# Gate and up products of a SwiGLU feed-forward by Strassen's seven block products, in a two-layer diffusion step on one Trainium2 core

## Chip, core and metric

The kernel runs on one core of one Trainium2 chip. The metric is the device time of one execution in microseconds (us). The engines are named as the profile names them: PE (TensorE, matrix products), DVE (VectorE), ACT (ScalarE), POOL (GpSimd), SP (the engine whose queue issues the DMAs).

## What is computed

The reference runs a backbone of two layers over 128 context tokens and 512 latent tokens of width 1024. A layer has adaptive modulation, a token mixer of four kinds of heads, and a SwiGLU feed-forward of inner width 2816 between two RMS norms. Only the feed-forward matters here:

```python
D_FF = -(-8 * D_MODEL // (3 * 256)) * 256            # 2816
...
h2 = modulate(rmsnorm(x, g_pre_ffn))                 # 640 tokens x 1024, both groups of tokens
f = (silu(h2 @ w_ffn_gate) * (h2 @ w_ffn_up)) @ w_ffn_down
x = x + gate * rmsnorm(f, g_post_ffn)
```

All of it is in 32-bit floating point, with the same weights for both groups of tokens.

## The kernel before

Activations lie with features on the 128 partitions and the 640 tokens along the row, cut into two halves of 320 (`HW`). A factor of a matrix product is held as two tiles, `hi` (the value rounded to the fast format fp32r) and `lo` (the rest), and a product is three passes, hi·hi, hi·lo, lo·hi (`PASSES`). One "k" of a product (128 of the depth) is thus three matmuls of 128x128 by 320 columns, and a full depth of 1024 is 24.

**Feed-forward.** The 2816 inner features are 22 tiles of 128, taken in `GROUPS` of 4, 3, 3, 4, 4 and 4. For a tile, `ev_ffn` makes for each half the gate product (24 matmuls), SiLU on ACT, the up product (24), and `ev_act` multiplies on DVE and splits the result into hi and lo (`act`). After the tiles of a group, `dn` adds the group's share of the down projection to the running sum `z` (8 output tiles, 2 halves, 3 matmuls per inner tile), which DVE evicts (`ev_dn`). The first group runs half 0 of all its tiles before half 1, since half 1 of `h` comes later; the last group keeps two tiles and its down products for a pass by halves, so that half 0 can go through `boundary` (norm, residual, norm and modulation for the next layer) while PE works on half 1.

```python
PASSES = ((0, 0), (0, 1), (1, 0))
...
for gi, gn in enumerate(GROUPS):
    ...
    for k in range(early):
        hg, hu = stream.next(), stream.next()
        for half in range(2):
            yield from ev_ffn(hg, hu, acts[k], half)
        stream.done(hg, hu)
```

**Weights.** The class `Stream` goes through a fixed list `items`. A 512 KB tile is loaded into one of three `raw` buffers and split by `split` into an `hl` tile (hi by a cast on ACT or DVE, lo by a subtraction on DVE or POOL), in one of 3 + 5 buffers. `feed` splits ahead as long as buffers are free; `next` hands a split tile to the products and `done` gives it back. Products accumulate in five PSUM tiles (`acc_tile`, `wide[0] = 5`).

**The order.** The whole program is one list that a recording layer writes: `drive` steps the main line `bulk` and a set of side lanes, and `Clock` keeps an estimate of when each engine is free. `vg` and `copy` choose the engine (DVE or POOL, DVE or ACT) by that estimate. So each engine's order is fixed when the program is built.

**Modulation weights.** In layer 0 a side lane (`mod_slots`) loads 28 MB in pieces of 1 MB (`mraw`) and lets PE make 28 small products from them (`mod_mm`, 8 matmuls in the order, `mps`), two at a time, in between the matmuls of the feed-forward; `mod_end` follows one turn later.

All engine operations come from the recording layer's `call` and so have one line in the profile, L232 (L234 in the order of the changed kernel); they are told apart by tile names.

Of the kernel before, what the change touches and what calls it, by code (L numbers as in the profile page):

```python
# [17 lines left out]
KT = 8  # L18
# [117 lines left out]
BIAS_CP = -200.0  # L136
BIAS_START = (-2000.0, 2000.0)
# [195 lines left out]
def emit(ctx, tc, a, o):  # L333
# [186 lines left out]
    def mod_lane(n):  # L520
        for _ in range(n):
            l, c = modq.pop(0)
            rawlim[0] = 1
            while stream.nd - stream.ns > 1:
                yield POLL
            raws = mod_dma(l, c)
            yield clock.done(raws) + 500.0
            tb = mod_mm(raws)
            rawlim[0] = NRAW
            yield  # L530
            mod_end(l, c, tb)
            yield

    def mod_slots(n):

        mine = [modq.pop(0) for _ in range(n)]
        tbs = []
        for i in range(0, n, 2):
            two = mine[i:i + 2]
            while live[0] + 2 * len(two) > NSLOT:  # L540
                yield POLL
            raws = [[u5([128, 4, 256], "mraw") for _ in range(2)] for _ in two]
# [6 lines left out]
            tbs = [(*lc_, mod_mm(r)) for lc_, r in zip(two, raws)]  # L549
            free(2 * len(two))  # L550
        yield
        for t in tbs:
            mod_end(*t)


    ext = [None]
    items = []
    for l in range(DEPTH):
        for c, u in [(c, u) for c in ((0, 1, 2) if l == 0 else (0, 2, 1)) + (3, 4, 5, 6, 7) for u in range(2)] + [(9, 0), (8, 0), (8, 1), (9, 1), (10, 0), (10, 1)]:
            k, n = (4, 256) if c in VCH else (KT, 128)  # L560
            items.append((a["win"][l, c, u].rearrange("p (k n) -> p k n", n=n), k, n, int(l > 0 and (1 <= c <= 2 or (c == 3 and u == 1)))))
        for c in range(8):
            items.append((a["wout"][l, c], KT, 128, int(c >= 3)))
        kb = 0
        for gi, gn in enumerate(GROUPS):
            last = gi == len(GROUPS) - 1
            for k in range(2 * gn):
                items.append((a["wgu"][l, 2 * kb + k], KT, 128, int(k == 3 or k >= 6) if last else int(k >= 3)))
            t = a["wdn"].tensor
            for m in range(0, 8, 2):  # L570
                off = l * DFF * D + 128 * kb * D + m * 128 * gn * 128
                src = bass.AP(t, off, [[gn * 128, 128], [128 * gn * 128, 2], [1, gn * 128]])
                items.append((src, 2 * gn, 128, int(m < 6) if last else int(m >= 2)))
            kb += gn

    class Stream:


        def __init__(self):
            self.raw, self.hl, self.where = {}, {}, {}  # L580
            self.nd = self.ns = self.nu = 0
            self.limit = 0
            self.used = [0, 0]

        def load(self):
            while self.nd < self.limit and self.nd < len(items) and self.nd - self.ns < rawlim[0]:
                src, kt, n, _ = items[self.nd]
# [5 lines left out]
        def split(self, at_once=False):  # L593
            _, kt, n, where = items[self.ns]
            self.used[where] += 1
            raw = self.raw.pop(self.ns)
            hl = (ext[0] if where else ring).tile([128, 2, kt, n], F32R, tag="hl", name="hl", bufs=NHL[where])
# [4 lines left out]
            self.ns += 1  # L602
            self.load()

        def free(self):
            where = items[self.ns][3]
            return self.used[where] < NHL[where] and (not where or ext[0] is not None)

        def feed(self):

            self.load()
            if self.ns < self.nd and self.free():
                now = clock.now()
                if clock.avail(self.raw[self.ns]) <= now + AHEAD and (
# [3 lines left out]
        def next(self):  # L618
            self.load()
            while self.ns <= self.nu:  # L620
                assert self.free()
# [10 lines left out]
    NHL = (3, 5)  # L632
# [726 lines left out]
    def boundary(half, yt, sqs, xls, out_dma, nxt):  # L1359
# [32 lines left out]
        if nxt:  # L1392
# [8 lines left out]
            yield from skewed(ended(pre(k)) for k in range(KT))  # L1401
        free(2)


    def bulk():
# [117 lines left out]
        for l in range(DEPTH):  # L1523
# [97 lines left out]
            ext[0] = None  # L1621
            wide[0] = 2
            bias[0] = BIAS_MIX
            pctx.close()
# [108 lines left out]
            fctx = ExitStack()  # L1733

            def scanned():
# [3 lines left out]
                ext[0] = clock.pool(fctx.enter_context(tc.tile_pool(name=f"f{l}", bufs=1)))  # L1739
                wide[0] = 5  # L1740
# [43 lines left out]
            xls = yield from residual(0, xsrc)  # L1784
            spawn(boundary(0, yt, ssqs[0], xls, xn, (l, 2, hk, ("h2", l))))
# [5 lines left out]

            def second(l=l, yt=yt, ssqs=ssqs, xls=xls, xn=xn):
                yield from boundary(1, yt, ssqs[1], xls, xn, (l, 2, hk, ("h2", l)))
                free(5)

# [248 lines left out]
```

## Time and profile before

| | |
|---|---|
| median of 3 runs | 1710.83 us (1710.33 to 1711.54) |
| the profiled execution | 1710.81 us, of which its span 1708.7 us |
| mean granted TensorE clock | 0.988 |
| PE busy | 1640.4 us (96%) |
| DVE busy | 959.7 us (56%) |
| ACT busy | 602.1 us (35%) |
| POOL busy | 228.9 us (13%) |
| DMA | 188.14 MB, mean 110 GB/s |

The span runs from the first to the last instruction; 2.1 us of the execution lie outside it. Matmuls overlap in the pipe, so the busy mean of one (313 ns) is not its share of the time; that is read from the start times of neighbours in the timeline. Layer 0 reaches to about 880 us and layer 1 to the end; in each, the mixer comes first and the feed-forward fills the second part.

### The profile page before, as it was taken

The page shows a single profiled execution, that of the slowest core. Times are in us where ns is not written, and L with a number is a line of the kernel's source. Part 1 is how long each engine was busy: PE and PEld are TensorE (multiplying, and loading weights), DVE is VectorE, ACT ScalarE, POOL GpSimd, SP SyncE. Part 2 cuts the span into 40 slices and gives each one's busy share as a digit, 9 for nine tenths or more (in the row PEclk, how much of TensorE's full clock was granted, in tenths as well). Part 3 has the DMA queues.
Part 4 walks back from the last instruction along what each step waited for, and adds up shares of the span by engine and source line. Part 5 has one row for each costly group of instructions (what it writes and reads, how often), then busy time and mean ns, then how long its engine had stood idle before and what let it go on. Part 6 is the DMA issues. An engine that isn't in the chain of part 4 may idle for free.

```text
span 1708.7 us, 31121 instructions
## 1 busy us (share of the span) xinstructions
PE 1640.4 (96%) x12784; PEld 1539.0 (90%) x12784; DVE 959.7 (56%) x2032; ACT 602.1 (35%) x1322; POOL 228.9 (13%) x280
## 2 busy tenths in 40 slices
PE   4999999999999999999979998998999999999996
PEld 2888988998999999999979986788999999999996
DVE  5488767696334444343484588775962434343356
ACT  5346655564210101011443466655642110101022
POOL 0200142032000000000233000330320000100012
PEclk9999999999999999999989998999999999999998
DMA  9332221554755621222241311104412222222022
GB/s 370 130 127 92 93 88 63 179 164 151 265 179 204 219 87 63 86 67 76 90 152 53 100 46 41 56 33 130 161 56 90 90 69 99 74 74 75 25 93 93
DMA packets 79997, 188.14 MB, mean 110 GB/s; under 512 B 7632, under 2 KB 38256, under 8 KB 79856
## 3 DMA queue, kind: packets, MB, share of 16 engines
q1 hardware_dynamic: 79856, 186.17, 32.2%
q8 instruction: 100, 1.64, 0.4%
q14 instruction: 41, 0.34, 0.1%
HBM read 173.42 MB, written 12.71 MB: 109 GB/s over the span
## 4 chain that ended last, share of the span: by engine, by line
PE 87%; DVE 7%; ACT 3%; issue 1%; DMA 1%; POOL 1%; SPq 0%; ACTq 0%; DVEq 0%; POOLq 0%
PE acc L232 68%; PE acct L232 6%; PE mps L232 3%; DVE z L232 1%; PE nsp L232 1%; DVE hl L232 1%; PE nps L232 1%; PE rops L232 1%; PE gdps L232 1%; PE ntp L232 1%; PE nops L232 1%; PE gaps L232 1%; ACT r L232 1%; PE lrp L232 1%; DVE gE L232 1%
## 5 line engine op out<-in xcount | busy, mean ns | idle before, releaser
L232 PE MATMUL acc<-h,hl 128*128 128x320 f32 x6336 | 977.9, 313 | 18.1 <-ACT h L232 9.3
L232 PEld LDWEIGHTS acc<-h,hl 128*128 128x128 f32 x6336 | 936.7, 188 | 43.6 <-issue 15.9
L232 PE MATMUL acc<-act,hl 128*128 128x320 f32 x2112 | 315.1, 310 | 1.3 <-DVE act L232 1.2
L232 PEld LDWEIGHTS acc<-act,hl 128*128 128x128 f32 x2112 | 310.4, 188 | 4.8 <-issue 2.1
L232 ACT ACTIVATE sg<-acc 128x320 f32<-128x320 f32 x88 | 38.4, 436 | 592.6 <-PE acc L232 592.5
L232 DVE TENSOR_TENSOR sg<-sg,acc 128x320 f32<-128x320 f32 x88 | 42.9, 487 | 360.3 <-PE acc L232 335.8
L232 DVE TENSOR_TENSOR hl<-raw,hl 128x1024 fp32r<-128x1024 f32 (+1 forms) x178 | 214.3, 1226 | 9.8 <-ACT hl L232 7.1
L232 POOL TENSOR_TENSOR hl<-raw,hl 128x1024 fp32r<-128x1024 f32 (+1 forms) x18 | 41.2, 2289 | 724.9 <-ACT hl L232 723.8
L232 ACT ACTIVATE hl<-raw 128x1024 fp32r<-128x1024 f32 (+1 forms) x118 | 118.6, 1030 | 51.9 <-PE acc L232 44.1
L232 PE MATMUL acct<-hl,h 128*128 128x256 f32 x960 | 133.4, 291 | 0.0
L232 PEld LDWEIGHTS acct<-hl,h 128*128 128x128 f32 x960 | 119.9, 191 | 9.1 <-issue 6.4
L232 DVE TENSOR_TENSOR z<-z,acc 128x320 f32<-128x320 f32 x160 | 74.5, 484 | 86.3 <-PE acc L232 86.2
L232 DVE CAST hl<-raw 128x1024 fp32r<-128x1024 f32 (+1 forms) x78 | 53.6, 687 | 16.8 <-PE acc L232 14.7
L232 POOL TENSOR_TENSOR nB<-nT,cst 128x248 f32<-128x248 f32 (+2 forms) x32 | 19.8, 620 | 279.3 <-DVE nsp L232 147.3
L232 PE MATMUL mps<-mraw,ct 128*32 128x256 f32 x768 | 49.1, 386 | 0.7 <-DVE modb L232 0.6
L232 POOL TENSOR_TENSOR ssqz<-ssqz,sq 128x320 f32<-128x320 f32 x34 | 32.6, 957 | 112.3 <-ACT sq L232 109.4
L232 DVE TENSOR_TENSOR act<-sg,act 128x320 fp32r<-128x320 f32 x88 | 43.3, 492 | 3.0
L232 ACT ACTIVATE qbd<-gE 32x256 f32<-32x256 f32 (+1 forms) x80 | 30.6, 382 | 37.5 <-DVE gE L232 34.4
L232 DVE CAST act<-sg 128x320 fp32r<-128x320 f32 x88 | 38.1, 432 | 3.1
L232 PEld LDWEIGHTS mps<-mraw,ct 128*32 128x32 f32 x768 | 24.7, 110 | 13.8 <-issue 2.8
L232 POOL TENSOR_TENSOR h<-xl,h 128x320 fp32r<-128x320 f32 x32 | 29.8, 944 | 46.2 <-DVE h L232 22.8
L232 DVE STREAM_TRANSPOSE modb<-mps 128x256 f32<-128x256 f32 x48 | 21.1, 445 | 18.9 <-PE mps L232 18.8
(252 smaller groups left out, 1508.1 us busy)
## 6 DMA issues: line engine op xcount, KB each, us to landing
mraw<-in_wmod SPq DMA_DIRECT2D x96, 512.0 KB
raw<-in_wgu SPq DMA_DIRECT2D x88, 512.0 KB
raw<-in_win SPq DMA_DIRECT2D x44, 512.0 KB
raw<-in_wdn SPq DMA_DIRECT2D x32, 512.0 KB
raw<-in_wout SPq DMA_DIRECT2D x16, 512.0 KB
xl<-xd SPq DMA_DIRECT2D x12, 640.0 KB
raw<-in_wdn SPq DMA_DIRECT2D x16, 384.0 KB
xd<-y SPq DMA_DIRECT2D x32, 160.0 KB
```

The costliest lines, as they stand in the source:

```text
L232: x = fn(*args, **kw)
```

## The change

Gate and up of one feature tile together are a 2x2 block matrix (gate and up as the two blocks of features, the depth of 1024 in two halves) times a 2x2 block matrix of `h` (depth halves by token halves). For 16 of the 22 tiles of a layer (all of groups 2 to 5 and the first two of the last group) the eight block products are replaced by seven (`seven`), each over a depth of 512, that is 4 k or 12 matmuls.

- **Sums of weights.** A tile now has four split tiles in place of two: gate (`plain`), the second half of up (`second`, 512 wide, tile `hu`), the four sums and differences of halves (`sums`: four `raw<-raw` operations of 128x512, in place, then a split), and the last form of up (`plain`). Buffers are 3 + 3 + 2 half ones in this stage (`hpool("b", 3)`).
- **Sums of `h`.** `sums_of_h` makes four differences of 320-token blocks in the `xl` tiles, splits three into `th` tiles and writes the fourth over the half-1 columns of `h` for the first four k, once the first group is done with them. `second_block` puts the old contents back before half 1 of the last two tiles.
- **Evictions.** `seven` evicts each product to SBUF: a copy and seven additions on DVE (`u`, `sg`), SiLU from SBUF, and `act` as before.
- **Pools.** The split buffers outside the ring are taken anew at three points of a layer (`hpool` "a", "b", "c").
- **Modulation weights** are loaded and multiplied one at a time instead of in pairs, from two buffers of the new pool, after the first group.

```diff
-                        hg, hu = stream.next(), stream.next()
-                        for half in range(2):
-                            yield from ev_ffn(hg, hu, acts[k], half)
-                        stream.done(hg, hu)
+                        yield from seven(acts[k])
...
+            def product(w, k0, x):
+                ps = acc_tile()
+                for k in range(4):
+                    for i, (wi, xi) in enumerate(PASSES):
+                        PE.matmul(ps, lhsT=w[:, wi, k0 + k, :], rhs=x(xi, k), start=(k == 0 and i == 0), stop=(k == 3 and i == 2))
+                    yield
+                return ps
...
+                hg = stream.next()
+                ps = yield from product(hg, 0, b11)
+                copy(p, ps, BIAS_SNAP)
+                ps = yield from product(hg, 4, b21)
+                stream.done(hg)
+                add(s0, p, ps)
+                S.activation(out=s0, in_=s0, func=AF.Silu)
+                hu, hs = stream.next(), stream.next()
+                ps = yield from product(hs, 0, t2)
+                add(p, p, ps)
+                hs2 = stream.next()
+                ps = yield from product(hs2, 4, t1)
+                add(s1, p, ps)
+                ps = yield from product(hs2, 0, t3)
+                stream.done(hs2)
+                add(p, p, ps)
+                add(u1, s1, ps)
+                ps = yield from product(hu, 0, t4)
+                stream.done(hu)
+                add(p, p, ps)
+                act(s0, p, ac, h0)
+                ps = yield from product(hs, 4, b22)
+                stream.done(hs)
+                add(s1, s1, ps)
+                S.activation(out=s1, in_=s1, func=AF.Silu)
+                act(s1, u1, ac, h1)
...
+                g, u = self.raw[srcs[0]], raw
+                (g1, g2), (u1, u2) = ((t[:, 0:KT // 2], t[:, KT // 2:]) for t in (g, u))
+                for out, x, y, op in ((u2, u1, u2, ALU.add), (u1, g1, u1, ALU.subtract), (g1, u2, g1, ALU.subtract), (g2, g2, g1, ALU.subtract)):
+                    vg(out, x, y, op, BIAS_SUM)
+                raw = g
...
-            for lc_, r in zip(two, raws):
-                for q in range(2):
-                    dma(out=r[q], in_=a["wmod"][lc_[0], lc_[1], q])
-            yield max(max(clock.done(r) for r in raws) + 500.0, clock.now() + 2 * MODGAP)
+            raws = mod_dma(*lc_, hx[0], 2)
+            yield max(clock.done(raws) + 500.0, clock.now() + MODGAP)
```

Over the whole program PE gets 384 matmuls fewer (6336 products of `h` become 5952, of which 1152 read `th`); DVE's order grows from 2035 to 2513 operations, ACT's from 1285 to 1359, POOL's from 286 to 334, and SP's stays at 476.

**PE, a Strassen tile in layer 0** (`h_123` to `h_130` are the eight depth tiles of `h`, `th` the sums, `mraw` modulation weights). Before:

```order
L232 MATMUL acc<-h_130,hl 128x320 x3
L232 MATMUL acc<-h_123,hl 128x320 x3
L232 MATMUL mps_6407<-modb,cst 32x4 x4
L232 MATMUL mps_6413<-modb,cst 32x4 x4
L232 MATMUL mps<-mraw,ct 32x256 x16
L232 MATMUL acc<-h_124,hl 128x320 x3
L232 MATMUL acc<-h_125,hl 128x320 x3
L232 MATMUL acc<-h_126,hl 128x320 x3
```

Now, from the third product of a tile to the last:

```order
L234 MATMUL acc<-th,hl 128x320 x24
L234 MATMUL mps_6511<-modb,cst 32x4 x4
L234 MATMUL mps<-mraw,ct 32x256 x8
L234 MATMUL acc<-h_123,hl 128x320 x3
L234 MATMUL acc<-h_124,hl 128x320 x3
L234 MATMUL acc<-h_125,hl 128x320 x3
L234 MATMUL acc<-h_126,hl 128x320 x3
L234 MATMUL acc<-th,hu 128x320 x12
L234 MATMUL acc<-h_127,hl 128x320 x3
L234 MATMUL acc<-h_128,hl 128x320 x3
L234 MATMUL acc<-h_129,hl 128x320 x3
L234 MATMUL acc<-h_130,hl 128x320 x3
```

A product ends after four k instead of eight, and a modulation slot holds one product instead of two.

**DVE, tiles of layer 1** (`sg`, `u`: evicted products; `act`: the split result; `raw`, `hl`, `hu`: weights). Before, one tile, both halves, with one split of a weight between:

```order
L232 TENSOR_TENSOR sg<-sg,acc 128x320
L232 CAST act<-sg 128x320
L232 TENSOR_TENSOR act<-sg,act 128x320
L232 TENSOR_TENSOR hl<-raw,hl 128x1024
L232 TENSOR_TENSOR sg<-sg,acc 128x320
L232 CAST act<-sg 128x320
L232 TENSOR_TENSOR act<-sg,act 128x320
```

Now, in the middle of one tile:

```order
L234 TENSOR_TENSOR u<-u,acc 128x320
L234 TENSOR_TENSOR sg<-u,acc 128x320
L234 TENSOR_TENSOR u<-u,acc 128x320
L234 TENSOR_TENSOR u<-sg,acc 128x320
L234 TENSOR_TENSOR u<-u,acc 128x320
L234 TENSOR_TENSOR sg<-sg,u 128x320
L234 CAST act<-sg 128x320
L234 TENSOR_TENSOR act<-sg,act 128x320
L234 TENSOR_TENSOR hu<-raw,hu 128x512
L234 TENSOR_TENSOR raw<-raw 128x512 x4
L234 CAST hl<-raw 128x1024
L234 TENSOR_TENSOR hl<-raw,hl 128x1024
```

The evictions and the preparation of the next tile's weights now stand close behind one another in DVE's queue.

**PE, the end of layer 0** (`nps` is a norm's sum over features; the second one of half 0 and then the first row of layer 1). Before:

```order
L232 MATMUL acc<-h_130,hl 128x320 x3
L232 MATMUL acc<-act,hl 128x320 x72
L232 MATMUL nps<-ssqz,cst 128x320 x2
L232 MATMUL acc<-act,hl 128x320 x24
L232 MATMUL acc<-h_123,hl 128x320 x3
L232 MATMUL nps<-ssqz,cst 128x320 x2
L232 MATMUL acc<-h_123,hl 128x320 x9
```

Now:

```order
L234 MATMUL acc<-h_130,hl 128x320 x3
L234 MATMUL acc<-act,hl 128x320 x21
L234 MATMUL nps<-ssqz,cst 128x320 x2
L234 MATMUL acc<-act,hl 128x320 x75
L234 MATMUL acc<-h_123,hl 128x320 x3
L234 MATMUL nps<-ssqz,cst 128x320 x2
L234 MATMUL acc<-h_123,hl 128x320 x9
```

The norm of half 0 stands 51 matmuls earlier among the last down products of half 1.

## Rows read from the trace of the kernel before

**Rows 1.** Page, busy time by engine: us, share of span, instructions.

```profile
PE 1640.4 (96%) x12784; PEld 1539.0 (90%) x12784; DVE 959.7 (56%) x2032; ACT 602.1 (35%) x1322; POOL 228.9 (13%) x280
```

**Rows 2.** Busy time by engine in two stretches of the feed-forwards, columns as headed.

```profile
core 0: us, PE busy (x) PEld busy (x) DVE busy (x) ACT busy (x) POOL busy (x), PEclk, DMA share, GB/s
468.00:616.00 148.00, 148.00 (x1354) 137.57 (x1353) 66.11 (x149) 17.68 (x26) 6.14 (x3) 1.00 0.55 195
1313.00:1640.00 327.00, 327.00 (x2231) 327.00 (x2231) 130.05 (x222) 43.62 (x64) 15.79 (x7) 1.00 0.24 78
```

**Rows 3.** Timeline of PE, layer 1: start, length (us), operation, count.

```profile
1439.69 56.48 PE L232 MATMUL acc<-h,hl 128*128 128x320 f32 x384
1496.01 28.32 PE L232 MATMUL acc<-act,hl 128*128 128x320 f32 x192
1524.17 56.48 PE L232 MATMUL acc<-h,hl 128*128 128x320 f32 x384
```

**Rows 4.** Timeline of PE, layer 0's feed-forward with modulation products.

```profile
476.60 0.31 PE L232 MATMUL mps<-modb,cst 128*32 128x4 f32 x16
476.74 1.94 PE L232 MATMUL mps<-mraw,ct 128*32 128x256 f32 x32
478.61 12.58 PE L232 MATMUL acc<-h,hl 128*128 128x320 f32 x84
491.12 0.31 PE L232 MATMUL mps<-modb,cst 128*32 128x4 f32 x16
```

**Rows 5.** Timeline of PE around a single modulation product in layer 0's mixer.

```profile
153.08 2.46 PE L232 MATMUL acc<-h,hl 128*128 128x320 f32 x15
155.47 1.08 PE L232 MATMUL mps<-mraw,ct 128*32 128x256 f32 x16
156.48 2.02 PE L232 MATMUL acc<-h,hl 128*128 128x320 f32 x12
```

**Rows 6.** Timeline of PE at layer 0's end; brackets: idle before, and releaser.

```profile
869.29 1.24 PE L232 MATMUL nps<-ssqz,cst 128*128 128x320 f32 x4
870.12 3.92 PE L232 MATMUL acc<-act,hl 128*128 128x320 f32 x24
882.68 0.63 PE L232 MATMUL acc<-h,hl 128*128 128x320 f32 x1 [8.64 <-ACT h L232]
```

**Rows 7.** Timeline of DVE at the same place.

```profile
878.92 1.22 DVE L232 TENSOR_TENSOR hl<-raw,hl 128x1024 fp32r<-128x1024 f32 x1
880.06 0.48 DVE L232 SCALAR_TENSOR_TENSOR r<-nps,r 128x320 f32<-128x320 f32 x1
```

**Rows 8.** DVE groups, 1313 to 1640 us: busy us, mean ns; idle before, releaser.

```profile
L232 DVE TENSOR_TENSOR hl<-raw,hl 128x1024 fp32r<-128x1024 f32 x37 | 44.3, 1222 | 0.8 <-ACT hl L232 0.2
L232 DVE TENSOR_TENSOR z<-z,acc 128x320 f32<-128x320 f32 x64 | 29.6, 485 | 41.3 <-PE acc L232 41.3
L232 DVE TENSOR_TENSOR act<-sg,act 128x320 fp32r<-128x320 f32 x32 | 15.7, 492 | 1.1
...
L232 DVE CAST hl<-raw 128x1024 fp32r<-128x1024 f32 x17 | 11.7, 686 | 0.0
L232 DVE CAST act<-sg 128x320 fp32r<-128x320 f32 x32 | 10.5, 327 | 1.2
```

**Rows 9.** DVE and POOL groups of the whole span, 512 wide.

```profile
L232 DVE TENSOR_TENSOR gE<-gE,gqk 128x512 f32<-128x512 f32 x28 | 19.3, 690 | 0.2 <-ACT gE L232 0.2
...
L232 POOL TENSOR_TENSOR rk<-rk,rope 128x512 f32<-128x512 f32 x4 | 5.1, 1282 | 8.3 <-ACT rdec L232 6.8 <-PE rrot L232 1.5
```

**Rows 10.** Timelines of DVE and of POOL at 1239.7 us.

```profile
1239.74 2.53 DVE L232 CAST act<-sg 128x320 fp32r<-128x320 f32 x1
...
1239.68 2.41 POOL L232 TENSOR_TENSOR hl<-raw,hl 128x1024 fp32r<-128x1024 f32 x1 [1.12 <-DMA xd<-y]
```

**Rows 11.** SP's queue from 419.51 us, then busy time by engine, 420 to 428.

```profile
419.51 2.26 SPq L232 DMA_DIRECT2D mraw<-in_wmod  x4
...
420.00:428.00 8.00, 8.00 (x63) 7.59 (x56) 2.93 (x6) 2.80 (x4) 0.00 (x0) 1.00 0.91 329
```

More of the change, by code (lines that the diff above doesn't have):

```diff
@@ L602, in split, with loaded @@
             self.ns += 1
+            for _ in range(ends):
+                self.raw.pop(self.nr)
+                self.nr += 1
             self.load()
         def free(self):
-            where = items[self.ns][3]
-            return self.used[where] < NHL[where] and (not where or ext[0] is not None)
+            where, when = jobs[self.ns][3:]
+            return self.used[where] < self.size[where] and (not where or (hx[0] is not None and when == stage[0]))
+        def loaded(self):
+            return self.ns < len(jobs) and jobs[self.ns][1][-1] < self.nd
         def feed(self):
             self.load()
-            if self.ns < self.nd and self.free():
+            if self.loaded() and self.free():
                 now = clock.now()
-                if clock.avail(self.raw[self.ns]) <= now + AHEAD and (
+                if clock.avail(self.raw[jobs[self.ns][1][-1]]) <= now + AHEAD and (
                         self.ns - self.nu < 2 or max(clock.t["V"], clock.t["S"]) <= now + BACKLOG):
@@ L1733, in bulk, with hpool @@
             fctx = ExitStack()
+            hctx = [None]
+            def hpool(nm, n):
+                if hctx[0] is not None:
+                    assert not stream.used[1] and not stream.used[2]
+                    hctx[0].close()
+                hctx[0], stage[0] = ExitStack(), nm
+                hx[0] = clock.pool(hctx[0].enter_context(tc.tile_pool(name=f"h{nm}{l}", bufs=1)))
+                stream.size[1] = n
             def scanned():
@@ new lines, in second_block @@
+            def second_block(l=l, hk=hk):
+                t = u5([128, 2, TOK], "tb")
+                for k in range(4):
+                    d, e = t[:, 0].rearrange("p (a n) -> p a n", a=2), t[:, 1, 0:HW]
+                    V.tensor_tensor(out=d, in0=hk[4 + k][:, :, HW:].bitcast(F32), in1=hk[k][:, :, HW:].bitcast(F32), op=ALU.subtract)
+                    yield
+                    vg(e, d[:, 0], d[:, 1], ALU.add)
+                    yield
+                    copy(hk[k][:, 0, HW:], e, BIAS_CP)
+                    yield
+                    vg(hk[k][:, 1, HW:], e, hk[k][:, 0, HW:].bitcast(F32), ALU.subtract)
+                    yield
+                free(1)
+                flags.add(("block", l))
@@ L1846, in bulk @@
                 if last:
-                    yield from room(1)
-                    sz = u5([128, 4, HW], "ssqz")
-                    ssqs = [[sz[:, i], sz[:, 2 + i]] for i in range(2)]
                     more = l + 1 < DEPTH
@@ L1877, in bulk @@
                     for half in range(2):
+                        if half:
+                            yield from until(("block", l))
                         for k in range(2):
```

150 lines of the change are left out of this document (118 added, 32 removed).

## The prediction

> **What bounds the kernel now.** I read the page's busy times first: PE is busy for 96% of the span, DVE for 56% [rows 1]. Such shares are means over stages, so the next view is the busy time in two stretches of the feed-forwards, where the change lies: there PE has no idle time at all (148.00 of 148.00 us and 327.00 of 327.00), at full granted clock, while DVE is busy for 40 to 45%, ACT for 12 to 13% and POOL for 4 to 5% [rows 2]. The reader should see that nothing but PE limits these stretches: a matmul removed there is time removed, as long as the work that the change hands to the other engines stays under PE's. Busy means of single matmuls overlap, so the price of one is taken from start times: 384 products of `h` from 1439.69 to 1496.01 us, 146.7 ns each, and 192 of the down projection from 1496.01 to 1524.17, 146.7 ns as well [rows 3].
>
> **The matmuls removed.** A Strassen tile needs 7 products of 4 k and 3 passes, 84 matmuls, where it had 2 x 2 x 8 x 3 = 96. With 16 such tiles in each of two layers that is 32 x 12 = 384 matmuls fewer, which the order confirms. 384 x 146.7 ns = **56.3 us less**. Does a shorter accumulation cost more for each matmul? Sums of the down projection already end after 9 or 12 matmuls, and they run at the same 146.7 ns [rows 3]. So I take nothing off.
>
> **Modulation products one at a time.** A pair with its closing matmuls costs PE, from one start to the next, 491.12 - 476.60 = 14.52 us, less 84 x 0.1467 = 12.32, so 2.20 us [rows 4]; 14 pairs are 30.8 us. A single one shows in the mixer: 15 matmuls from 153.08 end at 155.28 by the same pitch, the product starts at 155.47 and the next matmul at 156.48, so 1.20 us [rows 5]. Closing matmuls take 476.74 - 476.60 = 0.14 us for a pair [rows 4], 0.07 for one. 28 x 1.27 = 35.6 us: 4.8 us more. If a single one cost just half a pair it would be 0; I take **4 us more**, nearer to the row that shows a single one, and keep 0 to 5.
>
> **The work for DVE, ACT and POOL.** One tile before, on DVE: two weight splits of 1.22 us, part of their casts (0.69), and for each half a multiplication out of PSUM (0.49), a cast (0.33) and a subtraction (0.49) [rows 8]; some 5.7 us against 14.1 us of PE. One Strassen tile: seven additions out of PSUM (as `z<-z,acc`, 485 ns) 3.4; two multiplications 1.0; two casts 0.7; two subtractions 1.0; three full splits 3.7 and a half one 0.7 (priced as the 128x512 row, 690 ns); four sums of 512 2.8; about one and a half casts of weights 1.0 [rows 8, 9]. That is **14.2 us for DVE** if POOL takes none, against 84 x 0.1467 = 12.3 us of PE. So inside a run of tiles DVE has more to do than PE. A down projection gives it back: 28.2 us of PE for 16 additions and four splits, 14.1 us. A group of four is 4 x 14.2 + 14.1 = 70.9 us of DVE against 4 x 12.3 + 28.2 = 77.4 us of PE, 92%. Over this stage the DVE order of layer 1 adds up to 273 us at these prices, and POOL's to 41 us; PE has 2208 x 0.1467 = 324 us.
>
> Two things decide if a mean below 100% is enough. First, the lead of the weights: in the order every split of this stage stands behind the eviction of a product that is at least 8 products ahead of the one that reads it, 8 x 1.76 = 14 us, and up to 29 after a down projection. Four tiles in a row run up 4 x (14.2 - 12.3) = 7.6 us, which that lead holds. Second, the PSUM tiles: five, so PE goes on for four products, 7.0 us, past an uncollected one. The densest run of DVE between two evictions (the piece of the order shown) is 0.49 + 0.33 + 0.49 + 0.69 + 4 x 0.69 + 0.69 + 1.22 = 6.7 us [rows 8, 9]; it begins 1.8 us before the product in question ends, so that one waits for 5.4 us, 1.6 us inside the limit. ACT's new work (SiLU from SBUF, half splits) is hidden by its 87% of idle time. If this cover went, each tile would stretch towards 14.2 us; that is a rival below. For seams (three changes of pool in a layer, and behind a group's last product a chain of add, SiLU, multiply, cast and subtract where it was the last three) I set **2 us more**, with 0 to 10 as bounds: 0 since the down projection reaches the last tile's result only after 24 to 36 matmuls, 3.5 to 5.3 us, and three operations of that chain are 1.3 us [rows 8]; 10 if each of ten groups lost the 1 us that the chain grows by.
>
> The sums of `h` are some 22 DVE operations of 128x640 and their casts in each layer, while half 1 of the first group runs; what needs them comes after that group's 28.2 us of down products, with PE busy and DVE mostly free, so 0. The restoring of the block lies under half 0 of the last group, 0 too.
>
> **The end of layer 0.** PE stops for 8.64 us there: 24 matmuls follow the norm of half 0, then it waits until 882.68 for `h` of the next layer [rows 6], because DVE comes to that norm's result only at 880.06, behind the last evictions and a weight split that it began at 878.92 [rows 7]. In the new order the norm stands 51 matmuls (7.5 us) earlier in PE's stream, and DVE has its result before the last three evictions. But a cast and two subtractions of weight splits follow those evictions (0.69 + 2 x 1.22 us), and only then the second tile of `h`: about 7 us after PE's last down product, of which 2 us have matmuls. The stop becomes some 5 to 6 us; I take **3 us less**, with 8.6 less (all of it) and 3 more as ends.
>
> **Sum.** The profiled execution took 1710.81 us, 0.02 us from the median of the runs, so nothing has to be carried over. 1710.8 - 56.3 + 4 + 2 - 3 = 1657.5; I say **1657 us**. The parts' own ends reach from 1710.8 - 56.3 - 8.6 = 1645.9 to 1710.8 - 56.3 + 5 + 10 + 3 = 1672.5.
>
> **Rival 1: the vector engines take over the stage.** For it: POOL and DVE get in each other's way. A cast that takes 327 ns as a rule [rows 8] took 2.53 us at 1239.74, while a POOL subtraction of 2.41 us ran from 1239.68 [rows 10]. If DVE stood still for all of POOL's work, layer 1 would need 273 + 41 = 314 us for PE's 324, only 3% of room; ten per cent more for DVE's operations makes it 341, 17 us over, and layer 0 (286 + 44, then 359, for PE's 359 with the modulation products) just full. With the lead used up at the groups' ends, some 25 us in all: **1682 us**. Against it: the prices are already means of a stretch in which POOL worked for 15.8 us [rows 2, 8], and about a third of DVE's new load reads PSUM and has one operand in SBUF, for which no row shows a stop. Chance 0.12.
>
> The Trainium skill speaks for this rival: its page "SBUF — State Buffer" (section "SBUF: two separate sides") says that DVE and GpSimd share one pair of ports under an exclusive lock, so that the loser stands still for the whole instruction. The 2.53 us cast agrees with that. By it the time would be this rival's as soon as DVE's and POOL's work together fill the stage, and 1657 us as long as 314 us fit into 324.
>
> **Rival 2: slower, through the modulation loads in layer 0.** Each product waits for 1 MB that can be asked for only when the product before it has freed the two buffers. In the order 28 products stand 42 to 84 matmuls apart, the nearest 6.2 us. In the trace the four loads issued from 419.51 us moved, with a weight load, at 329 GB/s from 420 to 428 us [rows 11], 1.6 us for each 512 KB with their start: two take 3.2 us, with a weight ahead of them 4.8. That fits. But SP's queue is in order: a weight load that waits for its `raw` buffer holds the modulation load behind it, and the buffer now comes free only after the run of sums and a split, 5.4 us of DVE. The loss is 28 times the lateness; above 2.0 us on average (55 / 28) the gain is gone, at 3.5 us the time is 1657 + 98 = **1755 us**. Against it: the weight load is mostly issued behind the modulation load of its turn. Chance 0.04, a little of it at no change.
>
> **Rival 3: the change saves nothing since matmuls of four k run slower.** The down projection's pitch speaks against it [rows 3]: 1711 us, chance 0.02.
>
> **How the numbers follow.** My forecast, 1646 to 1666 us, has 0.76; rival 1 and longer seams, 1666 to 1705, 0.18 together (0.12 and 0.06); no change 0.02, slower 0.04. The range reaches over the forecast's ends and the lower part of rival 1, 1648 to 1674. A measurement tells 0.2%, 3.4 us, from no change: faster 0.94, same 0.02, slower 0.04.
>
> **What would show it.** Right: 384 matmuls fewer at a pitch of 146.7 ns; PE without idle time through the Strassen stage; DVE there at 80 to 90% busy; PE's waits of the feed-forwards still all at layer 0's end, shorter. Wrong: PE waiting for `hl`, `hu` or for evictions `u`, `sg` (rival 1), PE waiting for `mraw` and SP's queue waiting for DVE in layer 0 alone (rival 2), or a pitch above 147 ns.

## The result and the profile after

The changed kernel takes 1691.0 us (1690.3 to 1691.7), the kernel before in the same comparison 1711.2: a ratio of 0.988 with a 95% interval of 0.986 to 0.990. The forecast was 1657 us with a range of 1648 to 1674: the sign was right, but of 54 us of gain 20 came, and the time lies outside the range. It lies among "rival 1 and longer seams, 1666 to 1705", which had 0.18, 9 us above the price of rival 1.

The profiled execution has a span of 1688.2 us (before 1708.7). First the parts of its page that answer to [rows 1], and four of the page's groups of weight preparation, on DVE and on POOL:

```profile
PE 1598.9 (95%) x12400; PEld 1485.6 (88%) x12400; DVE 1269.9 (75%) x2510; ACT 637.6 (38%) x1396; POOL 307.4 (18%) x328
...
PE 71%; DVE 19%; ACT 4%; issue 3%; DMA 2%; POOL 1%; SPq 0%; DVEq 0%; ACTq 0%; POOLq 0%
...
L234 DVE TENSOR_TENSOR hl<-raw,hl 128x1024 fp32r<-128x1024 f32 (+1 forms) x204 | 251.4, 1241 | 12.6 <-ACT hl L234 8.5
...
L234 DVE CAST hl<-raw 128x1024 fp32r<-128x1024 f32 (+1 forms) x113 | 88.0, 779 | 20.1 <-PE acc L234 18.8
...
L234 POOL TENSOR_TENSOR hl<-raw,hl 128x1024 fp32r<-128x1024 f32 (+1 forms) x24 | 60.2, 2508 | 256.6 <-ACT hl L234 246.9
...
L234 POOL TENSOR_TENSOR raw<-raw 128x512 f32<-128x512 f32 x25 | 33.7, 1347 | 257.5 <-DVE hu L234 157.4
```

The same two rows of the page before, the chain and the casts on DVE:

```profile
PE 87%; DVE 7%; ACT 3%; issue 1%; DMA 1%; POOL 1%; SPq 0%; ACTq 0%; DVEq 0%; POOLq 0%
...
L232 DVE CAST hl<-raw 128x1024 fp32r<-128x1024 f32 (+1 forms) x78 | 53.6, 687 | 16.8 <-PE acc L232 14.7
```

The 384 matmuls are gone. In the chain of work that ended last DVE now holds 19%, before 7%. A cast of weights takes 779 ns where it took 687.

Next the busy time by engine between the stage marks of layer 1 (in turn a run of Strassen tiles and its down projection; columns us, PE, PEld, DVE, ACT, POOL, granted clock, DMA share, GB/s; the sum is over the eight stretches of the stage):

```profile
1304.57:1341.53 36.96, 36.96 (x254) 36.96 (x253) 29.65 (x53) 6.40 (x12) 1.30 (x1) 1.00 0.27 86
1341.53:1365.35 23.82, 21.35 (x146) 21.11 (x145) 19.46 (x31) 4.70 (x6) 6.15 (x3) 1.00 0.14 45
...
1426.68:1475.96 49.28, 49.28 (x338) 49.28 (x337) 41.72 (x73) 10.96 (x18) 7.60 (x4) 1.00 0.27 86
1475.96:1507.14 31.18, 28.43 (x195) 28.17 (x193) 25.48 (x39) 3.64 (x5) 5.49 (x3) 1.00 0.21 68
...
1557.41:1589.57 32.16, 30.19 (x194) 29.69 (x193) 26.08 (x39) 3.63 (x5) 6.63 (x3) 0.95 0.20 68
sum 285.00, PE 275.17 PEld 272.66 DVE 234.26 ACT 50.86 POOL 44.43; mean PE 34.40 PEld 34.08 DVE 29.28 ACT 6.36 POOL 5.55
```

and PE before, at a down projection of three tiles:

```profile
1355.21 21.28 PE L232 MATMUL acc<-act,hl 128*128 128x320 f32 x144
1376.33 42.40 PE L232 MATMUL acc<-h,hl 128*128 128x320 f32 x288
```

The reader should see two things first. A run of three tiles takes exactly 3 x 84 x 0.1467 = 36.96 us and one of four 49.28: inside most runs nothing is lost, and a matmul costs what it did [rows 3]. The time is lost in the down projections behind them: 23.82 us for 144 matmuls that took 21.12 before, 31.18 for 192 that took 28.16. And the busy times of DVE and POOL add up to 278.7 us in a stage of 285.0 (at least one of them is busy for 245.8).

A third thing is the granted clock of 0.95 in the last down projection. A piece of it, same columns:

```profile
1574.89:1578.30 3.41, 3.41 (x15) 3.41 (x14) 3.26 (x6) 0.63 (x1) 0.00 (x0) 0.50 0.44 175
```

For 3.41 us, right behind a stop of PE of 1.93 us, the clock is at half, 1.2 instead of 2.4 GHz, which loses some 1.7 us on top of the stop. The same stands behind stops of 1.50 us (until 519.61) and 1.84 us (until 762.06), and not behind those of 2.47 and 2.75 us. The three are some 5 us of the losses below.

The timeline at the first of these down projections, PE (bracket: idle before it, and what ended it):

```profile
1341.53 10.72 PE L234 MATMUL acc<-act,hl 128*128 128x320 f32 x72
1354.72 10.79 PE L234 MATMUL acc<-act,hl 128*128 128x320 f32 x72 [2.47 <-DVE z L234]
```

and DVE and POOL:

```profile
1343.77 0.49 DVE L234 TENSOR_TENSOR act<-sg,act 128x320 fp32r<-128x320 f32 x1
1344.18 1.22 DVE L234 TENSOR_TENSOR hl<-raw,hl 128x1024 fp32r<-128x1024 f32 x1
1345.31 0.68 DVE L234 TENSOR_TENSOR hu<-raw,hu 128x512 fp32r<-128x512 f32 x1
1346.03 2.87 DVE L234 TENSOR_TENSOR raw<-raw 128x512 f32<-128x512 f32 x4
1348.94 2.79 DVE L234 CAST hl<-raw 128x1024 fp32r<-128x1024 f32 x1
1351.76 1.23 DVE L234 TENSOR_TENSOR hl<-raw,hl 128x1024 fp32r<-128x1024 f32 x1
1352.91 3.90 DVE L234 TENSOR_TENSOR z<-z,acc 128x320 f32<-128x320 f32 x9
...
1348.70 2.48 POOL L234 TENSOR_TENSOR hl<-raw,hl 128x1024 fp32r<-128x1024 f32 x1 [29.41 <-ACT hl L234]
```

After the last tile's `act`, DVE has 8.7 us of preparation for the next tiles' weights before it collects the first product of the down projection. PE has made eight products by then (72 matmuls, nine for each) and stops for 2.47 us, until four evictions have run (1352.91 to 1354.7). Of these 8.7 us, 2.1 are a cast that takes 2.79 us instead of 0.69 while POOL's subtraction of 2.48 us runs.

To compare kernels below, the span is cut at four points of PE's timeline: A up to the first down projection of layer 0, B from there to the first product of layer 1, C from there to the first down projection of layer 1 (layer 1's mixer, which the change does not touch, its output projection and its first group), D from there to the last down projection. The rest is 28.6 us in both. By the forecast's terms A would change by -2.2 (one modulation pair moves from A into B), B by -28.2 + 6.2 - 3 + 1 = -24.0 (28 single products, 34.8 us, for 13 pairs, 28.6), C not at all, D by -28.2 + 1 = -27.2: 53.4 in all.

PE at these points, before (the start of C is the row of 882.68 in [rows 6]) and after:

```profile
432.48 0.60 PE L232 MATMUL acc<-act,hl 128*128 128x320 f32 x3
...
1284.81 15.42 PE L232 MATMUL acc<-act,hl 128*128 128x320 f32 x104
...
1680.12 14.24 PE L232 MATMUL acc<-act,hl 128*128 128x320 f32 x96
```

```profile
430.63 8.08 PE L234 MATMUL acc<-act,hl 128*128 128x320 f32 x54
...
870.11 0.64 PE L234 MATMUL acc<-h,hl 128*128 128x320 f32 x1 [6.20 <-ACT h L234]
...
1276.41 23.78 PE L234 MATMUL acc<-act,hl 128*128 128x320 f32 x161
...
1659.63 0.60 PE L234 MATMUL acc<-act,hl 128*128 128x320 f32 x3
```

| us | A | B | C | D | span |
|---|---|---|---|---|---|
| before | 432.5 | 450.2 | 402.1 | 395.3 | 1708.7 |
| after | 430.6 | 439.5 | 406.3 | 383.2 | 1688.2 |
| change | -1.9 | -10.7 | +4.2 | -12.1 | -20.5 |

So 13.3 us are missing in B, 15.1 in D, 4.2 in C and 0.3 in A, 32.9 together.

### The profile page after: what moved, and what is told of

Its sections match the earlier page's. It is cut to its first block, busy times and chain, and to the rows that moved or that the text cites. A ratio compares the mean times of both kernels' runs of the same rounds, so it can differ in the third digit from the quotient of the medians.

```text
span 1688.2 us, 31042 instructions
## 1 busy us (share of the span) xinstructions
PE 1598.9 (95%) x12400; PEld 1485.6 (88%) x12400; DVE 1269.9 (75%) x2510; ACT 637.6 (38%) x1396; POOL 307.4 (18%) x328
## 4 chain that ended last, share of the span: by engine, by line
PE 71%; DVE 19%; ACT 4%; issue 3%; DMA 2%; POOL 1%; SPq 0%; DVEq 0%; ACTq 0%; POOLq 0%
PE acc L234 52%; PE acct L234 6%; DVE hl L234 5%; PE mps L234 3%; DVE z L234 2%; DVE sg L234 2%; DVE act L234 2%; DVE raw L234 1%; PE nsp L234 1%; PE nps L234 1%; DVE u L234 1%; PE rops L234 1%; DMA raw<-in_wdn 1%; PE gdps L234 1%; ACT sq L234 1%
## 5 line engine op out<-in xcount | busy, mean ns | idle before, releaser
L234 PE MATMUL acc<-h,hl 128*128 128x320 f32 x4800 | 764.8, 314 | 17.4 <-ACT h L234 8.4
L234 PEld LDWEIGHTS acc<-h,hl 128*128 128x128 f32 x4800 | 714.5, 189 | 46.5 <-issue 19.1
L234 PE MATMUL acc<-act,hl 128*128 128x320 f32 x2112 | 323.2, 313 | 12.1 <-DVE z L234 9.0
L234 DVE TENSOR_TENSOR hl<-raw,hl 128x1024 fp32r<-128x1024 f32 (+1 forms) x204 | 251.4, 1241 | 12.6 <-ACT hl L234 8.5
L234 PE MATMUL acc<-th,hl 128*128 128x320 f32 x768 | 118.7, 309 | 1.4 <-DVE hl L234 1.4
L234 PEld LDWEIGHTS acc<-th,hl 128*128 128x128 f32 x768 | 114.0, 188 | 2.4 <-DVE hl L234 1.9
L234 DVE CAST hl<-raw 128x1024 fp32r<-128x1024 f32 (+1 forms) x113 | 88.0, 779 | 20.1 <-PE acc L234 18.8
L234 DVE TENSOR_TENSOR raw<-raw 128x512 f32<-128x512 f32 x103 | 71.0, 689 | 18.3 <-POOL raw L234 15.7
L234 DVE TENSOR_TENSOR u<-u,acc 128x320 f32<-128x320 f32 x96 | 46.4, 483 | 29.9 <-PE acc L234 27.6
L234 PE MATMUL acc<-th,hu 128*128 128x320 f32 x384 | 61.6, 309 | 0.0
L234 PEld LDWEIGHTS acc<-th,hu 128*128 128x128 f32 x384 | 57.6, 188 | 0.4 <-issue 0.4
```

The costliest lines, as they stand in the source:

```text
L234: x = fn(*args, **kw)
```

## The experiments

Three theories stood at first. **A:** the evictions of a down projection queue on DVE behind weight preparation, and PE has too few accumulators. **B:** DVE stands still beside POOL. **C:** DVE simply has too much to do.

**More accumulators, later weights, POOL off, casts to ACT.** The four edits, each alone on the changed kernel:

```diff
# e1
-                wide[0] = 5
+                wide[0] = 7
# e2: set at the end of a group's last tile, cleared after the first four evictions
+            if self.hold and self.ns - self.nu >= 4:
+                return
# e3
-BIAS_SUM = 0.0
+BIAS_SUM = 1e9
-BIAS_FFN = (BIAS_VS, BIAS_VG)
+BIAS_FFN = (BIAS_VS, 1e9)
# e4
-BIAS_FFN = (BIAS_VS, BIAS_VG)
+BIAS_FFN = (-3000.0, BIAS_VG)
```

> Seven accumulators in PSUM instead of five in the feed-forward, nothing else. Theory A (the evictions of the down projections stand on DVE behind the next tile's weight preparation; the first four products of a down projection are computed side by side, so five accumulators let PE go on for one product only, 1.76 us): PE may now go on for three products, 5.3 us, so the stops at the start of the down projections (1.6 to 4.0 us at each of eight, some 23 us together) mostly go: about 1671 us, and PE's waits for z (9.0 us in the trace after) fall below 2. Theory B (DVE is late since its casts stand still beside POOL): the delay stays and is only bridged in part, 1680 to 1688. Theory C (DVE has simply too much to do over the stage): more accumulators only put the stop off, over 1686.

Measured: 1691.5 us, ratio to before 0.987 (0.984 to 0.989), no gain (B 439.7, D 381.3). The premise was wrong, as the PE rows above show: PE already had eight products' lead there. In the kernel two of the five accumulators have a buffer each, and the other three are taken in turn from six (`mx`), so a larger `wide[0]` adds no buffer.

> From the end of a group's last Strassen tile until the first four evictions of its down projection are issued, no weights are prepared once four products' worth lie ready; five accumulators as before. The weight work ahead of the first eviction falls from 2.6 to 6.6 us to 0 to 1.2 us, and comes behind four evictions. Theory A: the stops at the start of the down projections go, 1671 to 1677 us. Theory B: the locks are where they were, within 4 us of 1691. Theory C: DVE idles for some 4 us at each seam, which it cannot spare, and PE waits for hl in the next tiles instead: 1691 to 1700.

Measured: 1683.3 us, 0.983 (0.981 to 0.985), between what theories A and B gave. B falls to 431.6, but D only to 382.0: one of the old stops stays (2.42 us), and the work came back as a stop of 4.18 us behind the first product of the next group, in which the granted clock falls to half, for 6.83 us. In DVE's timeline ahead of that stop POOL is again the reason, in three rows:

```profile
1413.95 0.69 DVE L234 TENSOR_TENSOR raw<-raw 128x512 f32<-128x512 f32 x1 [1.74 <-POOL hu L234]
1416.05 1.42 DVE L234 TENSOR_TENSOR raw<-raw 128x512 f32<-128x512 f32 x2 [1.41 <-POOL raw L234]
1417.51 2.72 DVE L234 CAST hl<-raw 128x1024 fp32r<-128x1024 f32 x1
```

> In the feed-forward the weights' subtractions and sums all go to DVE, none to POOL (24 subtractions and some 25 sums move). Theory A: DVE gets about 24 x 1.24 + 25 x 0.69 = 47 us more work and more of it ahead of the evictions, less what it no longer loses beside POOL: slower by 5 to 15 us, 1696 to 1706. Theory B: what DVE loses beside POOL is the cause, so faster by 10 to 15 us, 1676 to 1681. Theory C: slower by 15 or more, over 1706.

Measured: **1665.6 us**, 0.972 (0.971 to 0.974): 25 us faster than the change and better than any of the three theories gave, though DVE has 43 instructions more (2553). B is 430.2, C 402.1, D 373.3; 19.2 us of the gain lie in B and D, 4.2 in C. PE's clock is at its full level throughout from a layer's first down projection to its last. The same stage of layer 1 as above, in sum:

```profile
1328.34:1349.94 21.60, 21.38 (x146) 21.11 (x145) 20.62 (x34) 4.69 (x6) 0.00 (x0) 1.00 0.17 55
...
sum 275.43, PE 272.50 PEld 271.06 DVE 235.91 ACT 55.39 POOL 0.00; mean PE 34.06 PEld 33.88 DVE 29.49 ACT 6.92 POOL 0.00
```

DVE is busy for 235.9 us with POOL at nothing, and was for 234.3 with POOL at 44.4. So with POOL's 44 us DVE was busy for only 1.6 us less (in this kernel four of its casts, 2.7 us, went to ACT besides).

> In the feed-forward the planner gives the casts of the weights to ACT (1.03 us each there) instead of mostly to DVE. Theory A: 0.7 us less ahead of the evictions at each seam and a little less DVE load: 3 to 6 us faster, 1685 to 1688. Theory B: the casts are the instructions that stand still beside POOL (2.79 us in place of 0.69), so this takes the loss away: 10 to 15 us faster, 1676 to 1681. Theory C: DVE loses some 80 us of work over both layers, 15 to 25 us faster, 1666 to 1676.

Measured: 1701.8 us, 0.993 (0.991 to 0.995), slower than the change by 11 us (B 439.1, C 413.6, D 387.4), of which 7.3 lie in C and 3.8 in B and D together; all three theories were wrong here. DVE's own waits in the whole span suggest why nothing was gained: its order is fixed, and the subtraction that needs ACT's cast holds everything behind it. No run takes this apart further.

```profile
DVE hl L234 <- ACT hl L234: 130.5, 101, 6.5
```

**POOL as such.** Two ways in which POOL can hurt were left: DVE stands still while POOL runs (B1), or DVE's next instruction waits for POOL's result (B2). The first kernel adds useless POOL work to the kernel without POOL's share, and two others give back one part of that share:

```diff
# e5, on e3: at the end of each Strassen tile of layer 1
...
+                for _ in range(2 if l else 0):
+                    x = ac[:, 0, 0:512].bitcast(F32)
+                    nc.gpsimd.tensor_tensor(out=scr[0], in0=x, in1=x, op=ALU.add)
# e6, on the change
+BIAS_SUM = 1e9
# e7, on the change
+BIAS_FFN = (BIAS_VS, 1e9)
```

> The kernel with all weight preparation on DVE (1665.6 us), its DVE order unchanged, with 32 useless POOL additions of 128x512 (some 1.3 us each, 43 us in all, about POOL's work in layer 1 of the changed kernel) in layer 1, two behind each Strassen tile; nothing waits for them. Theory B1 (a DVE cast or subtraction stands still while POOL works): DVE is stretched by about a third of POOL's time, 14 us, in the place where the evictions queue: 5 to 10 us slower in layer 1, 1671 to 1676 us. Theory B2 (POOL costs time only where DVE's next instruction waits for POOL's result): 1664 to 1668.

Measured: 1691.3 us, 0.988 (0.986 to 0.990). D is 398.5 instead of 373.3: 25.2 us from 45 us of work whose results nobody reads, far over the 5 to 10 expected, and longer than before the change. (One cast on ACT waits 3.5 us for it at a change of pool, and some 6.8 of the 25.2 us are lost in four stretches of 3.41 us at half the granted clock.) DVE where the useless additions run, at the same down projection:

```profile
1331.29 2.06 DVE L234 TENSOR_TENSOR hl<-raw,hl 128x1024 fp32r<-128x1024 f32 x1
1333.27 1.52 DVE L234 TENSOR_TENSOR hu<-raw,hu 128x512 fp32r<-128x512 f32 x1
```

1.22 and 0.68 us in the kernel without them. PE's stop behind it grows from 0.22 to 3.19 us. B1 is shown, with DVE's order unchanged.

> The changed kernel with only the four sums of a tile's weights kept on DVE; POOL keeps its 24 or so subtractions (60 of its 94 us of weight work). Theory B2 (in the chain of four sums DVE waits in order for the sum that POOL has, 15.7 us in the trace after): most of the 25 us that came back with all work on DVE comes back here, 1666 to 1673. Theory B1: only the third of POOL's work that is gone counts, 1680 to 1686.

Measured: 1691.7 us, 0.988 (0.986 to 0.990): no gain, against both theories (B 435.9, D 388.5; some 8.5 us of D are lost at half the granted clock).

> The changed kernel with only the weights' subtractions kept on DVE; POOL keeps its 25 or so sums (34 of 94 us). Theory B1: two thirds of the gain, 1671 to 1677. Theory B2: the waits between the sums stay, 1687 to 1692.

Measured: 1672.1 us, 0.976 (0.974 to 0.979). B (429.4) and D (374.1) are those of the kernel without POOL; so it is the 24 subtractions of 2.5 us (and three half ones), not the 25 sums, that the change pays for. B2 falls as the main cause. The 23 sums that POOL still has here read SBUF too, 30 us, but DVE mostly waits for their results while they run (9.1 us of waits in layer 1), and in layer 1's stage none of its casts of weights or subtractions coincides with one.

**Reading or working?** The same place in the program, but POOL only writes (one column is read, so that it starts at the same time):

```diff
# e14, on e3, in the place of e5's additions
+                if l:
+                    x = ac[:, 0, 511:512].bitcast(F32)
+                    nc.gpsimd.tensor_tensor(out=scr[0][:, 0:1], in0=x, in1=x, op=ALU.add)
+                for _ in range(8 if l else 0):
+                    nc.gpsimd.memset(scr[0], 0.0)
```

> As the run with useless POOL additions, DVE's order again that of the kernel with all weight preparation on DVE (layer 1 from the first down projection to the last: 373.3 us, with the additions 398.5), but behind each Strassen tile of layer 1 POOL now reads one column from SBUF and then does eight MEMSETs of 128x512, which only write. If POOL's reading from SBUF is what stops DVE's two-operand instructions: no stretch, 373 to 377 us for that part and 1664 to 1670 in all (DVE's casts may still be held). If any work of POOL on SBUF does: as with the additions in proportion to POOL's time, 390 us or more.

Measured: 1675.1 us, 0.978 (0.976 to 0.979); D 381.3, neither of the two figures. Of its 8.0 us over the kernel without POOL work, 6.0 lie in the last group, whose weights' first cast on ACT waits 6.2 us for the last MEMSETs (they hold the pool that it takes over). Up to that group D is 305.6 us, against 303.6 without POOL work and 323.9 with the additions. DVE's and POOL's groups in that stretch, first with MEMSETs:

```profile
L234 DVE TENSOR_TENSOR hl<-raw,hl 128x1024 fp32r<-128x1024 f32 (+1 forms) x58 | 68.7, 1186 | 2.0 <-ACT hl L234 0.9
L234 DVE TENSOR_TENSOR z<-z,acc 128x320 f32<-128x320 f32 x63 | 27.3, 483 | 6.3 <-PE acc L234 6.3
L234 DVE CAST hl<-raw 128x1024 fp32r<-128x1024 f32 (+1 forms) x28 | 20.4, 730 | 5.6 <-PE acc L234 5.1
...
L1946 POOL MEMSET scr<- 128x512 f32 x112 | 63.6, 568 | 6.5
```

then with additions:

```profile
L234 DVE TENSOR_TENSOR hl<-raw,hl 128x1024 fp32r<-128x1024 f32 (+1 forms) x58 | 75.2, 1299 | 1.7 <-ACT hl L234 0.6
L234 DVE TENSOR_TENSOR z<-z,acc 128x320 f32<-128x320 f32 x63 | 27.3, 480 | 7.3 <-PE acc L234 7.3
L234 DVE CAST hl<-raw 128x1024 fp32r<-128x1024 f32 (+1 forms) x28 | 21.5, 767 | 5.6 <-PE acc L234 5.1
...
L1944 POOL TENSOR_TENSOR scr<-act 128x512 f32<-128x512 f32 x28 | 40.1, 1433 | 260.9 <-DVE act L234 259.8
```

Without POOL the means of the three are 1185, 481 and 682 ns. A subtraction of two SBUF operands is stretched by 40 us of POOL's additions and not at all by 64 us of its MEMSETs; the cast by both. The additions never coincide with an eviction `z`, so its row shows nothing here; in the changed kernel's stage of layer 1 19 of these evictions, with one operand in PSUM, ran beside a POOL subtraction, at 479 ns.

**Was POOL's share as dear before?**

```diff
# e10, on the kernel before
-BIAS_FFN = (BIAS_VS, BIAS_VG)
+BIAS_FFN = (BIAS_VS, 1e9)
```

> The kernel before, with the weights' subtractions of the feed-forward all on DVE as well. There DVE is busy for 40 to 45% of that stage and PE never stops in it. Theory B1 (POOL hurts only where DVE has no time to spare): nothing to gain, 1707 to 1714 us, and layer 1's stretch from the first down projection to the last stays at 395.3 us. Rival (POOL's share costs the kernel before as much, so it has nothing to do with the change): some 15 to 20 us faster, 1690 to 1697.

Measured: 1722.7 us, 1.006 (1.004 to 1.008). The two stretches answer: B 449.4 and D 395.3, as before, so POOL's share, here 17 subtractions, cost nothing while DVE had time to spare. The total does not, since C grew by 13.0 to 415.2 us. The edit moves a single subtraction there, near its end, and all of the loss stands before it; the planner sets the mixer's order by its estimated clocks, which any earlier edit shifts. PE's longest wait in C, of which the kernel before has none over 3 us:

```profile
PE acc L232 <- ACT h L232: 9.4, 1, 9.4
```

C was between 400 and 416 us in all these kernels. Totals of kernels with different orders are therefore compared by B and D.

**What is left with all preparation on DVE.** e9 sets `wide[0]` to 6 in the stage of the Strassen groups. e13 leaves the loop over the four sums out. e12 is e2's edit on e3, e11 hands weights over in single instructions, e15 is e11 repaired, e16 is e15 and e12 together:

```diff
# e11, e15
...
                     vg(out, x, y, op, BIAS_SUM)
+                    yield
                 raw = g
             copy(hl[:, 0], raw, BIAS_VS if at_once else bias[0][0])
+            yield
             vg(hl[:, 1], raw, hl[:, 0].bitcast(F32), ALU.subtract, 2000.0 if at_once else bias[0][1])
...
```

> All weight preparation on DVE, and six accumulators in place of five in the stage of the Strassen groups. If what is left over the forecast in the feed-forwards of the kernel with all of it on DVE (some 4 us in layer 1 and as much in layer 0, at the down projections) is still the queue of evictions on DVE, 1.8 us more of lead takes half of it: 1660 to 1664 us. If it is the load of DVE over the stage: 1664 to 1667.

> All weight preparation on DVE, but the four sums of a tile's weights are left out (what is multiplied is not Strassen's), so 32 x 2.8 = 88 us of DVE's work is gone, and the blocks ahead of the evictions shrink to 1.2 to 3.1 us. If the rest of the loss in the feed-forwards is DVE's load or its queue: that rest goes, 6 to 10 us, 1656 to 1660. If it lies elsewhere (pool changes, the last group's norm): under 3 us, 1663 to 1666.

> All weight preparation on DVE, and each weight prepared in single instructions (four sums, cast, subtraction) with the planner free to put an eviction between any two. If the rest of the loss in the feed-forwards (6.2 us in layer 1, 4 in layer 0 over the products that are left out) comes from evictions behind unbroken blocks of preparation of 4.7 to 6.6 us: those stretches shrink by 3 to 6 us together, 1660 to 1663 us in all. If not: within 2 us of 1665.6.

> All weight preparation on DVE, and none of it between a group's last Strassen tile and the first four evictions of its down projection once four weights lie ready. If the rest of the loss is the block of 4.7 to 6.6 us ahead of those evictions: 3 to 6 us less in the feed-forwards, 1660 to 1663. If DVE cannot spare the 5 us that it then idles: waits for weights in the next tiles, 1666 to 1675.

> The edit of the run with weights prepared in single instructions, repaired: that one left out two early weight preparations of the mixers, which cost 13 us before the first feed-forward. All weight preparation on DVE. Queue theory: the feed-forwards as there, 428.5 and 370.6 us (430.2 and 373.3 with unbroken blocks), the rest as in the kernel with all on DVE: 1659 to 1663 us. If the rest of the loss has nothing to do with blocks: 1664 to 1668.

> Both ways to keep evictions from queueing: single instructions, and no weight preparation between a group's last tile and the first four evictions of its down projection. All of it on DVE. Queue theory: the parts add up as far as there is something left over the products left out (367.1 us in layer 1): 427 and 369 to 370 us, 1657 to 1661 in all. If the idle time that the hold leaves on DVE is paid later: no better than one of the two, 1661 to 1668.

Measured (times are medians, stretches of the profiled execution):

| | us | ratio to before (95%) | B | C | D |
|---|---|---|---|---|---|
| e3, all on DVE | 1665.6 | 0.972 (0.971 to 0.974) | 430.2 | 402.1 | 373.3 |
| e9, six accumulators | 1681.0 | 0.981 (0.980 to 0.983) | 429.5 | 415.7 | 374.3 |
| e11, single instructions | 1677.3 | 0.980 (0.978 to 0.982) | 428.5 | 401.5 | 370.6 |
| e12, hold | 1667.6 | 0.974 (0.972 to 0.976) | 427.5 | 407.5 | 371.2 |
| e13, no sums | 1664.1 | 0.972 (0.970 to 0.974) | 427.6 | 403.1 | 369.2 |
| e15, single instructions | 1666.7 | 0.974 (0.972 to 0.976) | 429.3 | 404.9 | 370.5 |
| e16, both | 1662.7 | 0.971 (0.970 to 0.972) | 427.9 | 405.5 | 369.2 |

e9 gains nothing in B or D; of its 15 us 13.6 are C. e11's edit also left out two early weight preparations of the mixers, so its A is 444.0 us instead of 430.9. As totals all of these missed what the queue theory gave, e12, e13 and e15 by 4 to 5 us, e16 by 2, and these four fell into the range of the other outcome; in B and D, where the orders can be compared, it holds: each way to let evictions pass takes 2 to 3 us from D and 1 to 3 from B, and both together reach what the kernel without any sums has. That is the rest of DVE's queue: 6.4 us. A stretch comes from one profiled execution of each kernel, so how far it varies is not measured; the steps of 1 to 3 us rest on their agreeing, and on PE's waits for `z`, `act` and weights, which are all gone between those marks in e13 and e16. **e16 has the lowest median, 1662.7 us**, 28 less than the change and 50 less than before, with the same computation; its interval overlaps e3's.

## Why the prediction was wrong

**The matmuls removed: right.** 384 fewer, and a run of three tiles takes 36.96 us, the pitch of 146.7 ns. No time was lost to the shorter sums, so rival 3 falls.

**The modulation products: right in price, 1 us over in sum.** One costs 1.28 us in the changed kernel (54 matmuls from 439.66 end at 447.58 by the pitch, the next sum starts at 448.86); 28 x 1.28 = 35.8, 5.0 more than the pairs' 30.8 where 4 was taken. PE never waited for a load of `mraw`: rival 2 falls.

**The seams: this step failed.** "I set 2 us more, with 0 to 10 as bounds" measured 28: B lacks 13.3 us, less 1.5 for layer 0's end and 1 for the modulation products, plus the 1 it was given, D lacks 15.1 plus 1. The step behind it is "it begins 1.8 us before the product in question ends, so that one waits for 5.4 us, 1.6 us inside the limit": it was made for the seven products of a tile alone, and with every duration undisturbed. (By its own terms the wait is 6.7 - 1.8 = 4.9 us, and PE's lead at a seam is eight products, not four; neither slip makes the loss.) At a seam the tile's own chain takes 2.65 us from its last product on, and 6.6 us of preparation stand behind it (one subtraction more than in that block). Undisturbed that makes the first eviction 9.2 us late. PE's ninth product starts when four evictions of 0.43 us have run, at 10.9 us, and the eight before it take 72 x 0.1467 = 10.6: the kernel without POOL's share stops for 0.22 us there. With the cast at 2.79 us the four are done at 13.1, and PE stops for 2.47.

**DVE's load: the sum was right, the use made of POOL was not.** 92% was forecast for a group of four; without POOL's share DVE is busy for 86% of the stage of layer 1, and for 82% with it. "The prices are already means of a stretch in which POOL worked for 15.8 us" was one of the two reasons to set rival 1 at 0.12. In that stretch POOL ran 7 instructions; after, 22 of them in 285 us, at the places where DVE had the most to do. At DVE's prices without POOL they spared it 12 x 1.185 + 10 x 0.691 = 21 us. In the same stretch DVE's own instructions grew by 15 us: 32 casts of weights by 131 ns, 46 subtractions by 49, 14 half subtractions by 151, 28 multiplications `sg<-sg,u` by 201 and 28 casts of `act` by 35. It waited 7.1 us more for POOL's sums. The sum of both, 22 us, is what was spared.

**Rival 1 was the mechanism, not its size or its place.** It had the loss begin where the work of both no longer fits into the stage. Added up, 278.7 of 285.0 us, with the standstill in it, the work still fits. The loss began before that point, at the seams, because with an eviction 2 us later PE finds no accumulator free. Its price was 25 us; POOL's share alone cost 19.2 in B and D (9.3 and 9.9), the 5 us lost at half the granted clock included. The rule of the Trainium skill that stood beside it ("SBUF — State Buffer", section "SBUF: two separate sides") goes further: an instruction with two SBUF inputs is held only against a GpSimd one that reads SBUF. The traces agree: 1186 ns beside MEMSETs, 1299 beside additions, 1185 without either.

**The end of layer 0: half right.** PE stops there for 6.20 and 1.23 us instead of 8.64 [rows 6] and 0.32: 1.5 us less, 3 were taken.

**Layer 1's mixer was not in the sum.** It lost 4.2 us, and in the experiments it moved by up to 14 with the planner's order (415.7 in e9). No row of before could price that; the range should have had it as a bound of its own. Why some of these orders are worse stays open beyond the waits named.

**The account:** of the 32.9 us missing between the two spans, 19.2 are POOL's share of the weight preparation, 6.4 the rest of DVE's queue at the seams, 4.2 the mixer, 1.5 layer 0's end and 1.0 the modulation products. Another 2.3 us of the seams' 28 are left in e16 as well; there PE waits 1.25 us in each layer for POOL's `ssqz` (sums of squares for the norm) behind the last group's down products of half 0, a stop that the kernel before does not have in B or D. That is 34.6, less the 2 that the forecast had set aside, and 0.3 in A. (The 34 us between forecast and median hold 0.5 us of rounding and 0.7 by which the profiled execution lies below the median.)

## What to carry to other kernels

When a change takes away DVE's spare time, do not count POOL's share in the same preparation as relief. With DVE at 40 to 45% of a stage that share cost this kernel nothing; with DVE at 82% the 22 POOL instructions spared DVE 21 us and held it up for 22, and with the rest of POOL's share they cost 9.9 us of D. Work out the lateness of the first eviction at the seams between stages, with disturbed durations, against the accumulators that are free there, and not in the middle of a run. Where a planner orders the program, compare stretches that both kernels share before trusting a difference of totals under 1%.

## What the runs showed that was not expected

32 POOL additions of 128x512, 45 us of work with no reader, cost 25.2 us between layer 1's first and last down projection; 128 MEMSETs of the same size, 72 us, cost 8.0, most of it at a change of pool. A cast on DVE of 0.69 us took 2.79 beside one POOL subtraction of 2.48. Behind three of PE's stops in the changed kernel's feed-forwards (1.50, 1.84 and 1.93 us), and not behind its longest (2.47 and 2.75), the granted clock was at half for 3.41 us. Moving 94 casts of weights from DVE to ACT (209 there instead of 115) made the kernel 11 us slower, 3.8 of them in the stages that can be compared: DVE then stood for 130.5 us waiting for ACT's halves in its own queue.
